# A two-block transformer step on one core: the operands of the 256-column products begin in the middle of a 64-byte line

## The chip, the cores and the metric

The kernel runs on one core of a Trainium2 chip. The core has TensorE (matrix products, PE in the profile, with the loads of the stationary operand listed apart as PEld), VectorE (DVE), ScalarE (ACT), GpSimd (POOL) and SyncE (SP, which here issues the loads). The metric is the device time of one execution in microseconds. The kernel before has a median of 2021.78 us in three runs (2020.27 to 2024.73).

## What is computed

Two transformer blocks on a sequence of 512 tokens with 1024 channels, all in fp32. Cut to the places that matter here:

```python
# block 1: three mixers behind one projection, then a gated FFN
proj = rmsnorm(x) @ w_in                        # pool input, q/k/v, cross q, three gates
merged = g0 * pool(...) + g1 * stick_breaking_attention(...) + g2 * cross_attention(...)
h = x + rmsnorm(merged @ w_out)
gu = rmsnorm(h) @ w_ffn_in                      # 1024 -> 2 x 2816
h = h + rmsnorm((silu(gu[:, :2816]) * gu[:, 2816:]) @ w_ffn_out)

# block 2, layer 0: gated recurrence (HGRN); layer 1: causal attention (MLA), 8 heads of 192
for layer in range(2):
    x = x + mixer[layer](rmsnorm(x))
    u = rmsnorm(x) @ w_up                       # 1024 -> 2 x 2816
    gate, up = split(conv3(u))                  # a causal convolution over 3 tokens
    x = x + (silu(gate) * up) @ w_down
```

So there are three FFNs. The causal attention adds a mask of 0 and -1e30 to its scores.

## The kernel before

**Products.** A product with fp32 precision is made of three float32r products on TensorE: each operand is split into a high part (a cast on ScalarE, line 63) and a low part (a subtraction on VectorE, line 66), and `mm3` (lines 114 to 116) multiplies high by high, high by low and low by high into the same PSUM bank. Each of them loads a stationary tile of 128 x 128 and streams 512 or 256 columns of a moving tile past it. Weights arrive as `raw` tiles (two buffers), and are split into tiles of the tag "w" (eight buffers): `whi` and `wlo` in `chunk`, `wu` in `seven`. Activations, transposed, are `XH` and `XL`, of 8 x 512 columns (`new_X`).

**Products over 256 columns.** The FFNs' up projections are done in part by a scheme that takes seven products of blocks where eight are usual (`seven`): sums of blocks of the weights (`u`, made on VectorE) meet sums of blocks of the activations. The sums of the activations are made once in `x_sums` and split into the tiles `xc` (eight buffers). One call of `seven` is 7 products of 4 x 3 TensorE products of 256 columns each; four of the seven take `xc` as moving operand, three take views of `XH` and `XL`. The first FFN does both halves (gate and up) by it, 20 calls; the other two do the gate by it, 10 calls each, and the up half by `projA`, over 512 columns, on the same `XH` and `XL`. The first pair of column blocks of each FFN runs in `projA_first`, in two halves of 256 columns, beside the normalisation that ends the mixer.

**Places in memory.** Pools lay tiles one behind the other in each of the 128 partitions. `fill` (line 81) takes some bytes at a pool's start, so that the tiles behind begin where they are meant to: 224, 320 and 224 bytes at the start of three pools (lines 364 to 366) and 480 in the pool of the causal attention (line 1245). With these, every operand of every TensorE product begins at a multiple of 64 bytes in its partition, the large ones at a multiple of 256.

**Masks.** The strict mask `negS` (for the stick-breaking attention of block 1) and the causal mask `negC` (for the attention of block 2) are both loaded at the start, cast, and kept to the end.

**Order.** The order on each engine follows the order in which the code issues, with a filler woven between the steps of a chain (`weave`); every engine works through its own row in order. Loads are issued by SyncE, each one waiting for its buffer to come free.

Of the kernel before, what the change touches and what calls it, by code (L numbers as in the profile page):

```python
# [10 lines left out]
F32 = mybir.dt.float32  # L11
F32R = mybir.dt.float32r
I32 = mybir.dt.int32
U8 = mybir.dt.uint8
AF = mybir.ActivationFunctionType
# [4 lines left out]
P = 128  # L20
D = 1024
S = 512
NT = S // P
KD = D // P
# [10 lines left out]
def kernel(ctx: ExitStack, tc: tile.TileContext, a: dict, out: bass.AP):  # L35
    nc = tc.nc
    uid = [0]

    def nm(s):
        uid[0] += 1  # L40
        return f"{s}_{uid[0]}"

    def pool(name, bufs=1, **kw):
        return tc.tile_pool(name=name, bufs=bufs, reuse_waits="tile", **kw)

    cp = ctx.enter_context(pool("cp"))
    wp = ctx.enter_context(pool("wp", bufs=2 * RING))
    gp = ctx.enter_context(pool("gp", bufs=2))
    sp = ctx.enter_context(pool("sp", bufs=6))
    sp_fill = ctx.enter_context(pool("sf"))  # L50
    yp = ctx.enter_context(pool("yp", bufs=6))
    ps = ctx.enter_context(pool("ps", space=PSUM))
# [5 lines left out]
    def row(s):  # L58

        return yp.tile([P, 512], F32, tag="y", name=nm(s))  # L60

    def act(out_, in_, func, **kw):
        return nc.scalar.activation(out=out_, in_=in_, func=func, **kw)  # L63

    def tt(out_, in0, in1, op):
        return nc.vector.tensor_tensor(out=out_, in0=in0, in1=in1, op=op)  # L66
# [10 lines left out]
    def load(dst, src):  # L77
        return nc.sync.dma_start(out=dst, in_=src)


    def fill(pool_, n):

        if n:
            nc.gpsimd.memset(pool_.tile([P, n // 4], F32, name=nm("fill")), 0.0)

    ident = cp.tile([P, P], F32, name="ident")
    mhalf = cp.tile([P, 8], F32, name="mhalf")
# [30 lines left out]
    def split(src, hi, lo):  # L118
        act(hi, src, AF.Copy)
        tt(lo, src, hi.bitcast(F32), ALU.subtract)  # L120
# [36 lines left out]
            if plain is not None:  # L157
                act(plain[:, hf * 4 : hf * 4 + 4, c0 : c0 + P], b.rearrange("p (k t) -> p k t", k=4), AF.Copy)

    def new_X(xp):  # L160
        return (
            xp.tile([P, KD, S], F32R, tag="XH", name=nm("XH")),
            xp.tile([P, KD, S], F32R, tag="XL", name=nm("XL")),
        )

    def open_pool(name, side="left"):
        g = tc.tile_pool(name=name, bufs=1, reuse_waits="tile", side=side)
        p_ = g.__enter__()
        return p_, lambda: g.__exit__(None, None, None)
# [3 lines left out]
    def run(g):  # L173
        for _ in g:
            pass
# [108 lines left out]
    def halves_of(T, j, l):  # L284
        return T.rearrange("p (c j) t -> p j c t", j=2)[:, j, :, l * 256 : (l + 1) * 256]

    def x_sums(X, plain, tmp, xp):

        B = {(j, l): halves_of(plain, j, l) for j in range(2) for l in range(2)}
        nT1, T3, nT2, T4 = (tmp[:, 2 * i : 2 * i + 2].rearrange("p k (u t) -> p (k u) t", u=2) for i in range(4))  # L290
        ops = {}

        def parts(key, src):
            t_ = [xp.tile([P, 4, 256], F32R, tag="xc", name=nm("xc"), bufs=8) for _ in range(2)]
            split(src, *t_)
            ops[key] = t_

        tt(nT1, B[0, 0], B[0, 1], ALU.subtract)
        parts("nT1", nT1)
        tt(T3, B[1, 1], B[0, 1], ALU.subtract)  # L300
        stt(nT2, T3, -1.0, B[0, 0], ALU.mult, ALU.subtract)
        parts("nT2", nT2)
        parts("T3", T3)
        stt(T4, nT2, -1.0, B[1, 0], ALU.mult, ALU.subtract)
        parts("T4", T4)
        for j, l in ((0, 0), (1, 0), (1, 1)):
            ops[j, l] = [halves_of(x_, j, l) for x_ in X]
        return ops

    def seven(w, col, ops, xp, dst, c21, done):  # L310

        A = []
        for i in range(2):
            raw = (wp, xp)[i].tile([P, KD, P], F32, tag="raw", name=nm("raw"), bufs=2)
            load(raw, w[:, col + i * P : col + (i + 1) * P].rearrange("(k p) n -> p k n", p=P))
            A.append([raw.rearrange("p (c j) n -> p j c n", j=2)[:, j] for j in range(2)])
        bY, bXZ = bank("Y"), bank("XZ")
        pY, pX, pZ = bY[:, :256], bXZ[:, :256], bXZ[:, 256:]  # L320
        lf, rt = slice(0, 256), slice(256, 512)

        def product(o, src, key, first):
            t_ = wp.tile([P, 2, 4, P], F32R, tag="w", name=nm("wu"))
            split(src, t_[:, 0], t_[:, 1])
            x_ = ops[key]
            for c in range(4):
                mm3(o, (t_[:, 0, c], t_[:, 1, c]), (x_[0][:, c], x_[1][:, c]), first and c == 0, c == 3, skip_group_check=True)

        def usum(a_, b_, o=None):  # L330
            if o is None:
                o = xp.tile([P, 4, P], F32, tag="u", name=nm("u"), bufs=2)
            tt(o, a_, b_, ALU.add)
            return o

        product(pY, A[0][0], (0, 0), True)
        act(dst[0][:, lf], pY, AF.Copy)
        yield 1
        u1 = usum(A[1][0], A[1][1])
        product(pX, u1, "nT1", True)  # L340
        u3 = usum(A[0][0], A[1][0], A[1][0])
        u2 = usum(u3, A[1][1])
        product(pY, u2, "nT2", False)
        act(dst[0][:, rt], pY, AF.Copy)
        product(pZ, A[0][1], (1, 0), False)
        tt(dst[0][:, lf], pZ, dst[0][:, lf], ALU.add)
        done(0, 0)
        product(pY, u3, "T3", False)
        act(dst[1][:, rt], pY, AF.Copy)
        stt(dst[1][:, rt], pX, -1.0, dst[1][:, rt], ALU.mult, ALU.subtract)  # L350
        done(1, 1)
        yield 1
        product(pY, A[1][1], "T4", False)
        c21(dst[1][:, lf], pY)
        product(pX, usum(u2, A[0][1], u2), (1, 1), False)
        tt(dst[0][:, rt], pX, dst[0][:, rt], ALU.add)
        done(0, 1)
# [3 lines left out]
    mem_in = a["mem"][0]  # L361
    w_in = a["w_in"][0]

    fill(cp, 224)
    fill(sp_fill, 320)
    fill(ctx.enter_context(tc.tile_pool(name="rf", bufs=1, reuse_waits="tile", side="right")), 224)
    RA, close_RA = open_pool("RA", "right")
    M, close_M = open_pool("mp")
    E1, close_E1 = open_pool("e1")
# [42 lines left out]

    negS_f = row("negS_f")[:, :P]
    load(negS_f, a["c_neg_strict"])
    negC_f = row("negC_f")[:, :P]
    load(negC_f, a["c_neg_causal"])
    identR = cp.tile([P, P], F32R, name="identR")
    act(identR, ident, AF.Copy)
    negS = cp.tile([P, P], F32R, name="negS")
    act(negS, negS_f, AF.Copy)  # L420
    negC = cp.tile([P, P], F32R, name="negC")
    act(negC, negC_f, AF.Copy)

    def copies(dst, n=S):
        def f(bs):
# [359 lines left out]
    H_, close_H = open_pool("hp")  # L785
    h = H_.tile([P, NT, D], F32, name="h")

    def out_proj(w, Y, nk, gpost, gnext, half0, nxt, plain=lambda: None, parts=None):

# [59 lines left out]
        if parts is None:  # L851
            g0 = projB(w, 0, Y, nk, d0)
            xpool = half0(g0)
            last = xpool is None
            Xn = None if last else new_X(xpool)
            run(g0)
            bs = [bank("B", f"c{t}") for t in range(NT)]
            for c in range(nch - RING):
                ch = getB(w, c, 512)
                for t in range(NT):  # L860
                    run(mmB(bs, t, c, ch, Y, nk))
            ends = [(bs, c, getB(w, c, 512), Y) for c in range(nch - RING, nch)]
        else:
            xpool = half0(None)
            last = xpool is None
            Xn = None if last else new_X(xpool)

            def pair_of(c):
                y_ = [parts.tile([P, 2, S], F32R, tag="xc", name=nm("yc"), bufs=8) for _ in range(2)]
                split(Y[:, 2 * c : 2 * c + 2], *y_)  # L870
                return y_

            b2 = [bank("B") for _ in range(NT)], [bank("B", f"c{t}") for t in range(NT)]
            bs = b2[1]
            for c in range(nch - 2):
                yc = pair_of(c)
                for hf in range(2):
                    ch = getB(w, c, hf * 512)
                    for t in range(NT):
                        run(mmB(b2[hf], t, c, ch, yc, nk, x0=2 * c))  # L880
            ycs = [pair_of(c) for c in (nch - 2, nch - 1)]
            ends = [(b2[hf], c, getB(w, c, hf * 512), ycs[c - nch + 2]) for hf in range(2) for c in (nch - 2, nch - 1)]
# [43 lines left out]
    def ffn_first(w):  # L926
        return lambda X_, pend: projA_first(
            w, (0, DFF), X_, (lambda b: sinks[0](b), lambda b: sinks[1](b)), pend, lambda: ff["mid"]()
        )


    w_fi = a["w_ffn_in"][0]
    for t in range(NT):
        load(h[:, t], x_in[t * P : (t + 1) * P])
    XA, close_XA = open_pool("xa")
    open_ff()
    X, steps = out_proj(
        a["w_out"][0], MG, KD, gain(a["norm_mix_post"][0]), gain(a["norm_ffn_pre"][0]),
        lambda g0: XA, ffn_first(w_fi), kept,
    )  # L940
    close_RA()

# [291 lines left out]
    )  # L1234


    L, close_L = open_pool("ml")
    g_c = gp.tile([P, 512], F32, tag="g", name=nm("g"))
    load(g_c[:, :256], a["mla_q_a_norm_2"][0].unsqueeze(0).to_broadcast([P, 256]))
# [2 lines left out]

    kr = L.tile([P, NT, 64], F32, name="kr")
    ssr = L.tile([P, NT], F32, name="ssr")
    fill(L, 480)
    cn = [None] * NT

    def c_norm(t, b, o):
# [249 lines left out]
```

## Time and profile before

| | kernel before |
|---|---|
| median of three runs | 2021.78 us (2020.27 to 2024.73) |
| the profiled execution | 2020.12 us |
| its span, first to last instruction | 2018.3 us |
| granted clock, mean | 0.997 of 2.4 GHz |
| TensorE busy | 1985.7 us, 98% of the span |
| VectorE busy | 1278.9 us, 63% |
| ScalarE busy | 960.2 us, 48% |

The span is cut into stages by what runs in them: the mixers of block 1 to 437 us, the first FFN's up projections to about 645, the recurrence from about 775 to 1095, the second FFN to about 1450, the attention to about 1656 and the third FFN to the end. "Busy" counts an instruction from its start to its end; the products on TensorE overlap each other, so their pace is read from the distance of their starts.

### The profile page before, as it was taken

What the parts mean: (1) busy time and instruction counts of PE and PEld (TensorE: products, weight loads), DVE (VectorE), ACT (ScalarE), POOL (GpSimd) and SP (SyncE); (2) the same over time, 40 slices, a digit from 0 to 9 for tenths busy, and PEclk for the clock granted to TensorE, in tenths of its full rate; (3) what the DMA queues carried; (4) which work ended last, traced back from release to release, by engine and by line L of the source; (5) the groups of instructions that cost most, each with busy time, mean ns of one, the idle gap of its engine ahead of it and who ended that gap; (6) DMA issues with size and microseconds to landing.
All of it is one profiled execution on the core that took longest, in us unless ns stands there. A gap on an engine that the chain in (4) does not pass through costs nothing.

```text
span 2018.3 us, 29724 instructions
## 1 busy us (share of the span) xinstructions
PE 1985.7 (98%) x11665; PEld 1717.8 (85%) x11665; DVE 1278.9 (63%) x2293; ACT 960.2 (48%) x1862; POOL 56.6 (3%) x88
## 2 busy tenths in 40 slices
PE   8999999999999999999999999999989999999999
PEld 6877788889999888888888999988877789999887
DVE  5664543489888326666556887853556459887632
ACT  5543452366555227333244555542367555555521
POOL 0000000000000000000010000000021000000000
PEclk9999999999999999999999999999999999999999
DMA  6232223324333322212212233233231123332322
GB/s 225 89 94 75 72 76 125 105 84 126 105 105 96 103 94 84 74 63 74 65 51 89 85 113 97 84 107 102 67 97 32 43 62 106 94 103 86 105 94 84
DMA packets 192482, 183.44 MB, mean 91 GB/s; under 512 B 6999, under 2 KB 159830, under 8 KB 192342
## 3 DMA queue, kind: packets, MB, share of 16 engines
q1 hardware_dynamic: 192342, 181.54, 29.0%
q8 instruction: 92, 1.51, 0.3%
q14 instruction: 48, 0.39, 0.1%
HBM read 179.42 MB, written 2.10 MB: 90 GB/s over the span
## 4 chain that ended last, share of the span: by engine, by line
PE 90%; DVE 4%; DMA 3%; ACT 2%; POOL 1%; issue 1%; SPq 0%; ACTq 0%; DVEq 0%; POOLq 0%
PE B L114 10%; PE B L116 10%; PE B L115 10%; PE A L114 9%; PE A L115 9%; PE A L116 9%; PE Y L114 4%; PE Y L116 4%; PE Y L115 4%; PE XZ L116 3%; PE XZ L114 3%; PE XZ L115 3%; PE hs L1108 2%; PE zt L92 1%; DVE wlo L66 1%; PE tr L92 1%
## 5 line engine op out<-in xcount | busy, mean ns | idle before, releaser
L66 DVE TENSOR_TENSOR wlo<-raw,whi 128x1024 fp32r<-128x1024 f32 (+2 forms) x217 | 257.3, 1188 | 335.7 <-ACT whi L63 335.1
L63 ACT ACTIVATE whi<-raw 128x1024 fp32r<-128x1024 f32 (+2 forms) x217 | 224.0, 1033 | 369.4 <-PE B L115 251.6
L114 PE MATMUL A<-XH,whi 128*128 128x512 f32 (+1 forms) x912 | 335.9, 369 | 0.0
L115 PE MATMUL A<-XL,whi 128*128 128x512 f32 (+1 forms) x912 | 330.4, 362 | 0.4 <-DVE XL L66 0.4
L116 PE MATMUL A<-XH,wlo 128*128 128x512 f32 (+1 forms) x912 | 329.3, 361 | 0.0
L114 PE MATMUL B<-whi,yc 128*128 128x512 f32 x528 | 205.8, 390 | 0.0
L115 PE MATMUL B<-wlo,yc 128*128 128x512 f32 x528 | 205.5, 389 | 0.0
L116 PE MATMUL B<-whi,yc 128*128 128x512 f32 x528 | 205.3, 389 | 0.0
L116 PEld LDWEIGHTS A<-XH,wlo 128*128 128x128 f32 x912 | 173.5, 190 | 26.4 <-issue 0.2
L114 PEld LDWEIGHTS A<-XH,whi 128*128 128x128 f32 x912 | 173.8, 191 | 23.8 <-ACT XH L63 0.2
L115 PEld LDWEIGHTS A<-XL,whi 128*128 128x128 f32 x912 | 173.9, 191 | 23.3 <-DVE XL L66 0.9
L114 PE MATMUL B<-whi,XH 128*128 128x512 f32 (+2 forms) x416 | 164.8, 397 | 0.9 <-ACT whi L63 0.9
L115 PE MATMUL B<-wlo,XH 128*128 128x512 f32 (+2 forms) x416 | 157.1, 378 | 1.1 <-DVE wlo L66 0.7
L116 PE MATMUL B<-whi,XL 128*128 128x512 f32 (+2 forms) x416 | 157.1, 379 | 0.0
L114 PE MATMUL Y<-xc,wu 128*128 128x256 f32 x480 | 136.0, 283 | 2.4 <-ACT g L63 2.1
L116 PE MATMUL Y<-xc,wu 128*128 128x256 f32 x480 | 135.8, 283 | 0.0
L115 PE MATMUL Y<-xc,wu 128*128 128x256 f32 x480 | 135.8, 283 | 0.0
L63 ACT ACTIVATE wu<-u 128x512 fp32r<-128x512 f32 x120 | 75.2, 628 | 98.5 <-PE A L115 61.9
L63 ACT ACTIVATE wu<-raw 128x512 fp32r<-128x512 f32 x160 | 98.8, 624 | 42.8 <-DMA raw<-in_ffn_w_up_dram 21.0
L114 PEld LDWEIGHTS B<-whi,yc 128*128 128x128 f32 x528 | 99.1, 188 | 20.8 <-issue 0.5
L116 PEld LDWEIGHTS B<-whi,yc 128*128 128x128 f32 x528 | 99.1, 188 | 20.6
L115 PEld LDWEIGHTS B<-wlo,yc 128*128 128x128 f32 x528 | 99.2, 188 | 20.2
(326 smaller groups left out, 4214.7 us busy)
## 6 DMA issues: line engine op xcount, KB each, us to landing
raw<-in_ffn_w_up_dram SPq DMA_DIRECT2D x88, 512.0 KB
raw<-in_w_ffn_in_dram SPq DMA_DIRECT2D x44, 512.0 KB
raw<-in_ffn_w_down_dram SPq DMA_DIRECT2D x44, 512.0 KB
raw<-in_w_in_dram SPq DMA_DIRECT2D x42, 512.0 KB
raw<-in_hgrn_w_in_dram SPq DMA_DIRECT2D x32, 512.0 KB
raw<-in_w_ffn_out_dram SPq DMA_DIRECT2D x22, 512.0 KB
raw<-in_w_out_dram SPq DMA_DIRECT2D x8, 512.0 KB
raw<-in_hgrn_w_out_dram SPq DMA_DIRECT2D x8, 512.0 KB
```

The source lines that it names most:

```text
L63: return nc.scalar.activation(out=out_, in_=in_, func=func, **kw)
L66: return nc.vector.tensor_tensor(out=out_, in0=in0, in1=in1, op=op)
L92: nc.tensor.transpose(dst_bank[:, k * P : (k + 1) * P], s_, ident)
L114: nc.tensor.matmul(out_, lhsT=sta[0], rhs=mov[0], start=first, stop=False, **kw)
L115: nc.tensor.matmul(out_, lhsT=sta[0], rhs=mov[1], start=False, stop=False, **kw)
L116: nc.tensor.matmul(out_, lhsT=sta[1], rhs=mov[0], start=False, stop=last, **kw)
L1108: nc.tensor.matmul(b[:, sl], lhsT=K[:, e, sl], rhs=Q[:, e, sl], start=True, stop=True)
```

## The change

The tiles `xc` and `wu` become views that begin 32 bytes into a tile that is 64 bytes longer (`wide`, with `HALF` = 8 elements of 4 bytes). The same is done to `XH` and `XL` where a call asks for it, which only the `out_proj` ahead of the first FFN does (`at=HALF`); there all products on them go over 256 columns. The `XH` and `XL` of the other FFNs, which products over 512 columns read too, stay where a tile begins. All tiles of the tag "w" share buffers, so `whi` and `wlo` lie in the longer ones too, at their start.

For the bytes that this takes, the pool `sp` of small tiles has five buffers instead of six, the two masks share a buffer (tag "neg"), so that the causal one is loaded and cast only at its mixer, and the fills shrink to 32 bytes each. The fill of 480 bytes in the attention's pool is dropped; some tiles behind it, operands of plain-fp32 products and of transposes, now begin at an odd multiple of 32 bytes. The operands of the products over 512 columns begin at multiples of 64 bytes, no longer all of 256.

```diff
-    sp = ctx.enter_context(pool("sp", bufs=6))
+    sp = ctx.enter_context(pool("sp", bufs=5))
...
-    def new_X(xp):
-        return (
-            xp.tile([P, KD, S], F32R, tag="XH", name=nm("XH")),
-            xp.tile([P, KD, S], F32R, tag="XL", name=nm("XL")),
-        )
+    HALF = 8
+
+    def wide(xp, tag, name, shape, at, **kw):
+        n = int(np.prod(shape))
+        t_ = xp.tile([P, n + 2 * HALF], F32R, tag=tag, name=name, **kw)[:, at : at + n]
+        ax = " ".join(f"a{i}" for i in range(len(shape)))
+        return t_.rearrange(f"p ({ax}) -> p {ax}", **{f"a{i}": v for i, v in enumerate(shape)})
+
+    def new_X(xp, at=0):
+        return tuple(wide(xp, t, nm(t), (KD, S), at) for t in ("XH", "XL"))
...
         def parts(key, src):
-            t_ = [xp.tile([P, 4, 256], F32R, tag="xc", name=nm("xc"), bufs=8) for _ in range(2)]
+            t_ = [wide(xp, "xc", nm("xc"), (4, 256), HALF, bufs=8) for _ in range(2)]
...
         def product(o, src, key, first):
-            t_ = wp.tile([P, 2, 4, P], F32R, tag="w", name=nm("wu"))
+            t_ = wide(wp, "w", nm("wu"), (2, 4, P), HALF)
...
-    fill(cp, 224)
-    fill(sp_fill, 320)
-    fill(ctx.enter_context(tc.tile_pool(name="rf", bufs=1, reuse_waits="tile", side="right")), 224)
+    fill(cp, 32)
+    fill(sp_fill, 32)
+    fill(ctx.enter_context(tc.tile_pool(name="rf", bufs=1, reuse_waits="tile", side="right")), 32)
...
-    negC_f = row("negC_f")[:, :P]
-    load(negC_f, a["c_neg_causal"])
...
-    negS = cp.tile([P, P], F32R, name="negS")
+    negS = cp.tile([P, P], F32R, tag="neg", name="negS")
...
-    negC = cp.tile([P, P], F32R, name="negC")
-    act(negC, negC_f, AF.Copy)
...
     X, steps = out_proj(
         a["w_out"][0], MG, KD, gain(a["norm_mix_post"][0]), gain(a["norm_ffn_pre"][0]),
-        lambda g0: XA, ffn_first(w_fi), kept,
+        lambda g0: XA, ffn_first(w_fi), kept, at=HALF,
     )
...
+    negC_f = row("negC_f")[:, :P]
+    load(negC_f, a["c_neg_causal"])
+    negC = cp.tile([P, P], F32R, tag="neg", name="negC")
+    act(negC, negC_f, AF.Copy)
     L, close_L = open_pool("ml")
...
-    fill(L, 480)
```

The products stand in the same order as before, but for a handful in the first 60 us. What moves is the causal mask. On ScalarE, at the hand-over from the second FFN to the attention, the casts of the last weights (`whi`), of the last two transposed blocks of `XH` and the first sums of squares (`cn`) stand in this order in the kernel before:

```order
L63 ACTIVATE XH_12553<-tr_13350 128x4x128
L63 ACTIVATE XH_12553<-tr_13357 128x4x128
L63 ACTIVATE junk_13377,ssa_13331<-h 128x512
L63 ACTIVATE whi_13465<-raw_13463 128x512
L63 ACTIVATE XH_12553<-tr_13431 128x4x128
L63 ACTIVATE XH_12553<-tr_13438 128x4x128
L63 ACTIVATE cn_13475,css_13476<-B_13399 128x256
```

And at the same place in the changed kernel:

```order
L63 ACTIVATE XH_12549<-tr_13346 128x4x128
L63 ACTIVATE XH_12549<-tr_13353 128x4x128
L63 ACTIVATE junk_13373,ssa_13327<-h 128x512
L63 ACTIVATE whi_13463<-raw_13461 128x512
L63 ACTIVATE negC<-negC_f_13383 128x128
L63 ACTIVATE XH_12549<-tr_13429 128x4x128
L63 ACTIVATE XH_12549<-tr_13436 128x4x128
L63 ACTIVATE cn_13473,css_13474<-B_13397 128x256
```

The mask's cast stands one place ahead of the casts of the last two blocks of `XH`. On SyncE's row of loads at the same hand-over (`raw` are weights of the attention's first projection, `gq` and `gk` small gains) the kernel before has

```order
L78 DMA raw_13463<-in_mla_w_in_dram 128x2x256
L78 DMA gq_13751<-in_mla_q_norm_dram 128x64
L78 DMA gk_13761<-in_mla_k_norm_dram 128x64
L78 DMA raw_13561<-in_mla_w_in_dram 128x2x320
L78 DMA raw_13567<-in_mla_w_in_dram 128x2x320
L78 DMA g_14048<-in_norm_ffn_dram 128x1024
```

and the changed kernel

```order
L78 DMA raw_13461<-in_mla_w_in_dram 128x2x256
L78 DMA gq_13749<-in_mla_q_norm_dram 128x64
L78 DMA gk_13759<-in_mla_k_norm_dram 128x64
L78 DMA raw_13559<-in_mla_w_in_dram 128x2x320
L78 DMA negC_f_13383<-in_c_neg_causal_dram 128x128
L78 DMA raw_13565<-in_mla_w_in_dram 128x2x320
L78 DMA g_14046<-in_norm_ffn_dram 128x1024
```

where the mask's load stands between two loads of weights.

## Rows read from the trace of the kernel before

**Rows 1.** The page's busy times by engine, and TensorE's granted clock in 40 slices.

```profile
PE 1985.7 (98%) x11665; PEld 1717.8 (85%) x11665; DVE 1278.9 (63%) x2293; ACT 960.2 (48%) x1862; POOL 56.6 (3%) x88
...
PEclk9999999999999999999999999999999999999999
```

**Rows 2.** The page's chain that ended last, by engine.

```profile
PE 90%; DVE 4%; DMA 3%; ACT 2%; POOL 1%; issue 1%; SPq 0%; ACTq 0%; DVEq 0%; POOLq 0%
```

**Rows 3.** TensorE's groups by form: count | busy us, mean ns of one | idle before.

```profile
L114 PE MATMUL Y<-xc,wu 128*128 128x256 f32 x480 | 136.0, 283 | 2.4 <-ACT g L63 2.1 <-ACT u L63 0.3
...
L114 PE MATMUL XZ<-XH,wu 128*128 128x256 f32 x320 | 90.6, 283 | 0.0
...
L114 PE MATMUL A<-XH,whi 128*128 128x256 f32 x256 | 74.3, 293 | 0.0
...
L1108 PE MATMUL hs<-Q,K 128*128 128x128 f32 x448 | 59.0, 274 | 0.0
...
L114 PE MATMUL XZ<-xc,wu 128*128 128x256 f32 x160 | 45.3, 283 | 0.0
```

**Rows 4.** Timeline of TensorE, first FFN: start us, length us, instruction; 168 steps.

```profile
579.79 0.28 PE L114 MATMUL Y<-xc,wu 128*128 128x256 f32 x1
579.91 0.28 PE L115 MATMUL Y<-xc,wu 128*128 128x256 f32 x1
...
599.95 0.28 PE L114 MATMUL Y<-xc,wu 128*128 128x256 f32 x1
```

**Rows 5.** Timeline of TensorE, last down projection, products over 512 columns; 67 steps.

```profile
1959.76 0.39 PE L115 MATMUL B<-wlo,yc 128*128 128x512 f32 x1
...
1974.95 0.39 PE L116 MATMUL B<-whi,yc 128*128 128x512 f32 x1
```

**Rows 6.** Timeline of TensorE, recurrence: plain-fp32 products over 128 columns, merged.

```profile
841.74 1.05 PE L1108 MATMUL hs<-Q,K 128*128 128x128 f32 x8
```

**Rows 7.** Timeline of TensorE, third FFN: from 512 columns to 256.

```profile
1696.55 0.39 PE L116 MATMUL A<-XH,wlo 128*128 128x512 f32 x1
1696.78 0.28 PE L114 MATMUL Y<-xc,wu 128*128 128x256 f32 x1
1696.89 0.28 PE L115 MATMUL Y<-xc,wu 128*128 128x256 f32 x1
1697.01 0.28 PE L116 MATMUL Y<-xc,wu 128*128 128x256 f32 x1
```

**Rows 8.** Timeline of all engines near 600 us: a weight load.

```profile
599.95 0.19 PEld L115 LDWEIGHTS Y<-xc,wu 128*128 128x128 f32 x1
```

**Rows 9.** Busy us by stretch: length, PE, PEld, DVE, ACT, POOL, clock, DMA.

```profile
437.00:500.00 63.00, 63.00 (x528) 63.00 (x527) 62.56 (x119) 40.19 (x76) 0.00 (x0) 1.00 0.34 102
500.00:645.00 145.00, 145.00 (x1211) 145.00 (x1210) 124.14 (x230) 85.24 (x168) 0.00 (x0) 1.00 0.33 99
1130.00:1310.00 180.00, 180.00 (x1123) 163.13 (x1122) 148.94 (x227) 100.60 (x166) 0.00 (x0) 1.00 0.34 104
```

**Rows 10.** Timeline of ScalarE: the mask's cast, and the hand-over to the attention.

```profile
22.54 0.31 ACT L63 ACTIVATE negC<-negC_f 128x128 fp32r<-128x128 f32 x1
...
1454.61 0.63 ACT L63 ACTIVATE whi<-raw 128x512 fp32r<-128x512 f32 x1
1458.66 1.33 ACT L63 ACTIVATE XH<-tr 128x512 fp32r<-128x512 f32 x2 [3.41 <-PE tr L92]
```

**Rows 11.** Timeline of SyncE's issues at the same hand-over.

```profile
1452.58 0.34 SPq L78 DMA_DIRECT2D gq<-in_mla_q_norm_dram  x1
1453.91 0.38 SPq L78 DMA_DIRECT2D raw<-in_mla_w_in_dram  x1
1456.74 0.38 SPq L78 DMA_DIRECT2D raw<-in_mla_w_in_dram  x1
```

**Rows 12.** Timeline of VectorE there: what waited for the small load.

```profile
1455.76 0.29 DVE L66 TENSOR_TENSOR tq<-cosT,gq 128x128 f32<-128x128 f32 x1 [0.62 <-DMA gq<-in_mla_q_norm_dram]
```

**Rows 13.** The strict mask's products: count, shortest/median/longest ns, first to last start us.

```profile
L521 PE MATMUL z<-negS,identR x32: 272/302/332, 53.3 to 232.7; 128*128 128x128 f32 x32
```

More of the change, by code (lines that the diff above doesn't have):

```diff
@@ L81, in fill @@
     def fill(pool_, n):
-        if n:
-            nc.gpsimd.memset(pool_.tile([P, n // 4], F32, name=nm("fill")), 0.0)
+        nc.gpsimd.memset(pool_.tile([P, n // 4], F32, name=nm("fill")), 0.0)
     ident = cp.tile([P, P], F32, name="ident")
@@ L786, with out_proj @@
     h = H_.tile([P, NT, D], F32, name="h")
-    def out_proj(w, Y, nk, gpost, gnext, half0, nxt, plain=lambda: None, parts=None):
+    def out_proj(w, Y, nk, gpost, gnext, half0, nxt, plain=lambda: None, parts=None, at=0):
         first = {}
@@ L854, in out_proj @@
             last = xpool is None
-            Xn = None if last else new_X(xpool)
+            Xn = None if last else new_X(xpool, at)
             run(g0)
@@ L865, in out_proj @@
             last = xpool is None
-            Xn = None if last else new_X(xpool)
+            Xn = None if last else new_X(xpool, at)
             def pair_of(c):
```

## The prediction

> **What bounds the kernel now.** I read the page's busy times and its chain first: TensorE is busy for 98% of the span [rows 1] and the chain that ended last runs through it for 90% [rows 2], at a granted clock of 1.00 in nearly every slice [rows 1]. So time comes or goes here almost only with the pace at which one product follows another. That pace is not in the groups of instructions: their 283 ns for a product over 256 columns is the length of one, and these overlap. The groups give the number and the kind [rows 3]. The pace is read from the starts in the timeline: in a stretch of products over 256 columns the starts at 579.79 and 599.95 us lie 168 steps apart, 120.0 ns each [rows 4]; over 512 columns those at 1959.76 and 1974.95 us lie 67 steps apart, 226.7 ns each [rows 5]. The difference, 106.7 ns for 256 columns, is one column per cycle of 2.4 GHz. What is left is the same in both, 120.0 - 106.7 = 13.3 ns per product, 32 such cycles. On this **excess** the prediction rests, since an operand's place in a line cannot change the columns.
>
> Two rows say what the excess is not. It is not the price of any change of the stationary tile: eight products of plain fp32 over 128 columns in 1.05 us, 274 ns long each [rows 3], follow each other at (1.05 - 0.27) / 7 = 111 ns [rows 6], and they too load 128 columns of 4-byte weights per product. So the load of a stationary tile allows 111 ns. Nor is it constant: the first product over 256 columns behind one over 512 starts at 1696.78 us, the next at 1696.89, and from there on the step is 0.12 again [rows 7]. With the same tiles at the same places a step of 0.11 us is possible when the work ahead was another. I read the excess as two readers of the same memory, the stream of moving columns and the load of the next stationary tile, which start at the same hundredth of a microsecond [rows 4, 8] and get in each other's way; the time at which each steps on to its next piece then matters, and so may the place where an operand begins.
>
> **The change, part by part.** In the kernel before every operand of every product begins at a multiple of 64 bytes (most at a multiple of 256). Afterwards the tiles xc and wu begin 32 bytes later, and XH and XL of the first FFN too. There are 3360 products of the seven-product scheme at 120 ns: 40 calls of `seven` times 84, which the groups add up to: three lines each of 480 and 320, six of 160, of which one each is shown [rows 3]. Of these 1680 are in the first FFN, with both operands shifted; in the two others 960 have both shifted (those on xc) and 720 only the stationary one (those on XH, XL). Of the 768 that TensorE runs on XH and XL with aligned weights (three lines of 256) [rows 3], the 192 of the first FFN's start have a shifted moving operand alone; the others keep their places.
>
> Both shifted, 2640 products. No row shows an operand off a multiple of 64, so the price is bounded from both sides. Below: 111 ns, the pace that the load of a stationary tile allows [rows 6], a gain of 9 ns each. Above: the excess is paid in pieces; if the 512 bytes of a stationary row are 8 lines of 64 bytes, a line costs 13.3 / 8 = 1.67 ns, a start in mid-line touches 9 lines instead of 8, and the moving row 17 instead of 16: 1.67 to 3.3 ns lost each. I take half of the excess back, 6.65 ns, since 106.7 + 6.65 = 113.3 ns is what the step of 0.11 us behind a product over 512 columns shows [rows 7], the nearest row there is. The reason is one of phase: the moving row is read at twice the rate of the stationary one, so with both begun in mid-line the first half line is used up after 8 cycles on the one side and 16 on the other, and the two no longer step on in the same cycle; begun at a line's start they do, every time.
>
> Not all of it reaches the end. From 437 to 500 us, where the first FFN's products run beside the angles of the rotary tables, VectorE is busy for 62.56 of 63.00 us [rows 9]: it cannot follow a faster TensorE there, and 63 / 0.120 = 525 products gain nothing. Behind that it is busy for 124.14 of 145.00 us and in the second FFN for 148.94 of 180.00 [rows 9], 86% and 83%: room for a TensorE that is 5.6% faster. So (2640 - 525) x 6.65 ns = **14.1 us less**.
>
> One shifted, 912 products: the phases differ by one half line in another way, and no row tells whether it helps. I take nothing; the ends are 9 ns gained and 1.67 ns lost, -8.2 to +1.5 us.
>
> Products over 512 columns keep places at a multiple of 64, though no longer of 256. In rows 5 the moving operand begins at a multiple of 512 bytes and the stationary one 256 further, and the products of rows 4, at other multiples of 256, have the same excess; odd multiples of 64 no row shows. I take nothing; a line's price each, 1.67 ns, would be 8.6 us on 5172 products. The plain-fp32 attention products of the second mixer, 144, and 144 transposes move to mid-line as well, because the fill of 480 bytes in their pool goes; the plain-fp32 pace of 111 ns [rows 6] is that of the loads, so I take nothing; at a full excess more for each they would cost 288 x 13.3 ns = 3.8 us.
>
> The causal mask. Its load, its row buffer and its cast leave the start (0.31 us of ScalarE at 22.54 us [rows 10]) and stand now in the hand-over to the second block's second mixer: on ScalarE ahead of the two casts of XH that TensorE waits for, on SyncE's load queue between two weight loads. In the trace those loads are issued at 1453.91 and 1456.74 us, each in 0.38 [rows 11]; the second waits for a buffer, so the mask's 64 KB would go out at about 1454.3. The small load issued at 1452.58 [rows 11] ended a wait of VectorE at 1455.76 [rows 12], 3.2 us later. The mask then lands at about 1457.5 and its cast ends at 1457.8. ScalarE is idle from 1455.2 until the casts at 1458.66, which wait for TensorE's transposes [rows 10]: the cast is hidden, with 0.8 us to spare. Without this cover it would cost what it is late, 0.3 us and more, with two casts of XH and the first sums of squares queued behind it. The buffer that the mask shares with the strict mask is last read at 232.7 us [rows 13], so nobody waits for it. Five instead of six small buffers in `sp`, and shorter fills: a small tile is written and read within a step or two of a loop, and I cost them at nothing. What comes late next in this hand-over is the load behind the cast, and it is not moved.
>
> The sum: 14.1 us less, all else nothing. The profiled execution took 2020.12 us around a span of 2018.3, so it would come to 2006.0; the median of the runs, 2021.78, lies 1.7 above it. From the median: 2021.8 - 14.1 = **2007.7 us**, said as 2008.
>
> A page would put the gain higher. The Trainium skill, "TensorE: Matmul & The Clock Gate", section Back-to-back issue gap, gives columns / 2.4 + 2.5 ns from product to product, 109.2 for 256; the trace has 120.0 instead, with loads between. If the shift brought that gap back, the sum would be 2115 x 10.8 ns = 22.8 us and the time 1999, an estimate by that page.
>
> **The rivals.**
> *Nothing changes.* The excess is a fixed price of handing the array from one 4-byte stream to the next, or the pieces read are 32 bytes or less. For it speaks that it is 13.3 ns at 256 and at 512 columns alike; against it, the step of 0.11 us [rows 7] and the 111 ns of rows 6. Time: 2022, within 2 us. The Trainium skill, "SBUF — State Buffer", section Specifications (TRN2), gives SBUF lines of 16 bytes; by that rule a row shifted by 32 bytes touches as many lines as before, and this rival holds. No row here shows a line's length.
> *A half line more is read.* The price of the upper bound above: 2640 x 3.3 + 912 x 1.67 ns = 10.2 us, at all 3552 products since TensorE is the bound there. Time 2032. It decides if the memory is read in lines of 64 bytes and each line costs its own collision, whatever the phase. For it speaks that 32 cycles divide evenly by 8 lines; if moving and stationary collide a second time per product, it would be as much again, 2042.
> *The whole gap closes* to 111 ns, for both kinds: (3552 - 525) x 9 ns = 27 us, 1995. Against it speaks VectorE, which at 86% would be near its limit.
> *The gain is bounded by VectorE* all through the first FFN: then only the 960 products of the other two gain, 6.4 us: 2015.
>
> **How the numbers follow.** Forecast (half the excess) 0.30, whole gap 0.10, VectorE as bound 0.10, nothing 0.22, a half line more 0.28. Faster by over 0.2% (about what a measurement of this kernel can tell from no change, 4 us): 0.50. Within: 0.22. Slower: 0.28. The range reaches from 1994 (whole gap) to 2036 (a half line more, and the mask or the small buffers some us late); of the slower case the part above it, with a second collision, is left out. If it is faster, 1994 to 2016.
>
> **What would show it.** In the profile after, the step between starts of products on xc and wu: 113 ns by the forecast, 120 by the first rival, 121.7 to 123.4 by the second, 111 by the third. The products on XH and wu of the second FFN tell the one-sided shift apart. The step of 512 columns must still be 226.7 ns, and VectorE's share from 500 us on must rise from 86 to some 90%. The mask's cast must stand before the casts of XH with idle time behind it. I am wrong if the step stays at 120.0 or grows, or if the step of 512 columns moves.

## The result and the profile after

The changed kernel is **slower by 0.68%**: 2035.7 us in the median (2034.74 to 2039.48) against 2022.67 us for the kernel before in the same comparison, a ratio of 1.0068 with a 95% interval of 1.0051 to 1.0086. The profiled execution took 2034.74 us around a span of 2032.8 us, 14.5 us more than the span before (2018.3).

Busy times, TensorE's clock and the chain, from the page of the changed kernel:

```profile
PE 2000.2 (98%) x11665; PEld 1713.2 (84%) x11665; DVE 1278.2 (63%) x2293; ACT 959.9 (47%) x1862; POOL 56.6 (3%) x87
...
PEclk9999999999999999999999999999999999999999
...
PE 88%; DVE 5%; ACT 2%; DMA 2%; issue 1%; POOL 1%; SPq 0%; POOLq 0%; ACTq 0%; DVEq 0%
```

Against [rows 1, 2] TensorE is busy for 14.5 us more, with the same 11665 products at the same clock; VectorE and ScalarE have not moved by 1 us. So the products follow each other more slowly. The same products as in [rows 4], 168 steps apart (start, length, instruction):

```profile
582.66 0.28 PE L113 MATMUL Y<-xc,wu 128*128 128x256 f32 x1
...
602.51 0.28 PE L113 MATMUL Y<-xc,wu 128*128 128x256 f32 x1
```

and as in [rows 5], 67 steps apart:

```profile
1973.35 0.40 PE L114 MATMUL B<-wlo,yc 128*128 128x512 f32 x1
...
1988.84 0.39 PE L115 MATMUL B<-whi,yc 128*128 128x512 f32 x1
```

Over 256 columns the step fell from 120.0 to 19.85 / 168 = **118.2 ns**. Over 512 columns, where no view was moved, it rose from 226.7 to 15.49 / 67 = **231.3 ns**. The steps also lost their evenness: before, nearly every product of 256 columns came 120 ns behind the last; afterwards nine in ten lie between 114 and 123 ns, in no fixed order. Counting the steps from start to start of all products by kind accounts for the whole difference:

| sum of the steps behind products | before | after | difference |
|---|---|---|---|
| on 512 columns (5171) | 1210.2 us | 1229.7 us | +19.5 |
| on 256 columns with `wu` (3360) | 405.7 | 401.0 | -4.7 |
| on 256 columns, others (1032) | 128.8 | 128.3 | -0.5 |
| the rest (plain fp32, transposes, waits between) | 261.7 | 262.0 | +0.3 |
| all | 2006.4 | 2021.0 | +14.6 |

The question is why products slow down whose views stayed at a tile's start.

### The profile page after: what moved, and what is told of

It reads as the page before. It is cut to its first block, busy times and chain, and to the rows that moved or that the text cites. A ratio compares the mean times of both kernels' runs of the same rounds, so it can differ in the third digit from the quotient of the medians.

```text
span 2032.8 us, 29733 instructions
## 1 busy us (share of the span) xinstructions
PE 2000.2 (98%) x11665; PEld 1713.2 (84%) x11665; DVE 1278.2 (63%) x2293; ACT 959.9 (47%) x1862; POOL 56.6 (3%) x87
## 4 chain that ended last, share of the span: by engine, by line
PE 88%; DVE 5%; ACT 2%; DMA 2%; issue 1%; POOL 1%; SPq 0%; POOLq 0%; ACTq 0%; DVEq 0%
PE B L113 10%; PE B L114 10%; PE B L115 10%; PE A L113 9%; PE A L114 9%; PE A L115 9%; PE Y L113 3%; PE Y L114 3%; PE Y L115 3%; PE XZ L114 3%; PE XZ L113 3%; PE XZ L115 3%; PE hs L1110 2%; PE zt L91 1%; PE tr L91 1%
## 5 line engine op out<-in xcount | busy, mean ns | idle before, releaser
L113 PE MATMUL B<-whi,yc 128*128 128x512 f32 x528 | 208.2, 394 | 0.0
L115 PE MATMUL B<-whi,yc 128*128 128x512 f32 x528 | 207.6, 394 | 0.0
```

Source lines behind the costliest of these rows:

```text
L113: nc.tensor.matmul(out_, lhsT=sta[0], rhs=mov[0], start=first, stop=False, **kw)
L115: nc.tensor.matmul(out_, lhsT=sta[1], rhs=mov[0], start=False, stop=last, **kw)
```

## The experiments

**The theories.** What did change for the 512-column products is where their tiles lie. The slots of the weight ring are 4160 bytes long instead of 4096, those of XH and XL 16448 instead of 16384, and the fills no longer round up to 256. Before, all of these operands stand at a multiple of 256; afterwards at 0, 64, 128 or 192 past one. *T1*: the pace hangs on how the places of the stationary and the moving operand stand to each other modulo 256; equal places give the even 226.7 and 120.0 ns, unequal ones more on 512 columns and less on 256. *T2*: the place inside a 64-byte line counts, the 32 bytes that the change is about. *T4*: the side edits (mask, sp, fills) cost the time. *T5*: not the places, but what ScalarE, VectorE or the transfers do beside them.

**The pace by itself (m1).** Streams of products and nothing else, all operands views of one long tile, `m` and `s` the bytes past a multiple of 256 of the moving and the stationary pair:

```python
for i in range(16):
    k = i % 8
    for u, v in ((0, 0), (0, 1), (1, 0)):                  # hi-hi, hi-lo, lo-hi
        nc.tensor.matmul(b[:, :n], lhsT=big[:, so[u] + k * 256 : so[u] + k * 256 + 128],
                         rhs=big[:, mo[v] + k * n : mo[v] + k * n + n], ...)
```

> This kernel leaves the two blocks out: it copies x to one long tile as fp32r and runs only streams of 48 products of 512 or of 256 columns in the pattern hi-hi, hi-lo, lo-hi, each with a weight load of 128x128, whose four operands lie at chosen numbers of bytes past a multiple of 256 within that tile; the four last streams of either width run beside copies on ScalarE and subtractions on VectorE. T1 (the pace hangs on how the addresses of the operands of one product, or of neighbouring products, stand to each other beyond 64 bytes): the streams with all operands at equal places show the 226.7 and 120.0 ns of before, those with 64, 128 or 192 bytes between operands show 230 to 233 ns and 114 to 118 ns. T2 (the place inside a 64-byte line counts): only streams whose operands lie at 32, 96, 160 or 224 differ from the others. T5 (the pace does not hang on the places of TensorE's own operands, but on what ScalarE, VectorE or the transfers do beside them): every stream without work beside it shows 226.7 and 120.0 ns, whatever the places.

The timeline of TensorE, merged; a stream's 48 steps end at the next stream's start. In the names, `wide` is 512 columns and `half` 256; M and S are followed by the places of the high and the low part, one letter for every 32 bytes: `a` is 0, `b` 32, `c` 64, `i` 256, `q` 512:

```profile
43.88 11.05 PE L56 MATMUL wideMaaSaax<-big 128*128 128x512 f32 x48
54.77 11.35 PE L56 MATMUL wideMaaSbbx<-big 128*128 128x512 f32 x48
65.96 11.36 PE L56 MATMUL wideMaaSccx<-big 128*128 128x512 f32 x48
77.16 11.40 PE L56 MATMUL wideMaaSddx<-big 128*128 128x512 f32 x48
...
132.95 11.04 PE L56 MATMUL wideMaaSiix<-big 128*128 128x512 f32 x48
143.83 11.04 PE L56 MATMUL wideMaaSqqx<-big 128*128 128x512 f32 x48
...
232.26 11.07 PE L56 MATMUL wideMbbSbbx<-big 128*128 128x512 f32 x48
243.16 11.25 PE L56 MATMUL wideMegSegx<-big 128*128 128x512 f32 x48
254.25 11.08 PE L56 MATMUL wideMaiSaix<-big 128*128 128x512 f32 x48
...
265.17 5.91 PE L56 MATMUL halfMaaSaax<-big 128*128 128x256 f32 x48
270.93 5.84 PE L56 MATMUL halfMaaSbbx<-big 128*128 128x256 f32 x48
276.60 5.82 PE L56 MATMUL halfMaaSccx<-big 128*128 128x256 f32 x48
282.26 5.79 PE L56 MATMUL halfMaaSddx<-big 128*128 128x256 f32 x48
...
389.90 11.36 PE L56 MATMUL wideBusyMaaSccx<-big 128*128 128x512 f32 x48
401.10 11.09 PE L56 MATMUL wideBusyMbbSbbx<-big 128*128 128x512 f32 x48
```

On 512 columns, equal places: 10.89 / 48 = 226.9 ns; the weights 32 bytes off 233.1, 64 bytes off 233.3; 256 bytes off 226.7 again. Both operands 32 bytes past a multiple of 256, and so equal: 227.1. On 256 columns: 120.0 at equal places, 118.1 at 32 bytes, 117.9 at 64. The other unequal pairs gave 229 to 234 ns on 512 columns and 117 to 120 on 256. So T1 has the directions; its sizes, 230 to 233 and 114 to 118 ns, were too narrow. T2 falls, since 64 acts as 32 does and a common 32 does nothing.

In the streams named `Busy` only VectorE was at work beside TensorE, not ScalarE as well. ScalarE's copies ran earlier, from 21 to 152 us, beside the first ten streams. Busy time of PE, PEld, DVE, ACT and POOL during `wideBusyMaaSccx`:

```profile
389.90:401.10 11.20, 11.20 (x49) 9.02 (x48) 10.89 (x10) 0.00 (x0) 0.00 (x0) 1.00 0.00 0
```

This stream, 64 bytes off, took 233.3 ns, as the one beside ScalarE did. T5 falls: `wideMegSegx`, with neither engine at work, took 11.09 / 48 = 231.0 ns, where T5 has 226.7.

**In the kernel (e1 to e3).** e1 is the changed kernel without the shift:

```diff
-        t_ = xp.tile([P, n + 2 * HALF], F32R, tag=tag, name=name, **kw)[:, at : at + n]
+        t_ = xp.tile([P, n + 2 * HALF], F32R, tag=tag, name=name, **kw)[:, 0:n]
```

> The changed kernel with every view moved back to the start of its tile: nothing lies at 32 bytes any more, but the tiles keep their 4160 and 16448 bytes, so that their places differ by multiples of 64 and not of 256. T1 (places that differ modulo 256 slow the products of 512 columns from 226.7 to about 231.5 ns and quicken those of 256 from 120.0 to about 118): as the changed kernel, 2031 to 2040 us, 512-column step 230 to 233 ns. T2 (the 32 bytes inside a line are what counts): back to before, 2019 to 2026 us, and the step on 256 columns back to 120.0 ns.

e3 is the kernel before with the side edits alone: `sp` with five buffers, the masks' move, and `fill(sp_fill, 352)`, which holds the places. The fill of 480 bytes in the attention's pool stays.

> The kernel before with only the side edits: causal mask loaded and cast where the changed kernel does it, in one shared buffer with the strict one, and five sp buffers; the fill behind sp is 352 bytes, so that all big tiles stay at a multiple of 256. T1 and T2: no difference, 2018 to 2026 us, steps 226.7 and 120.0 ns. T4: 2030 to 2040 us.

e2 is e3 with longer slots in the weight ring:

```diff
-            t_ = wp.tile([P, 2, 4, P], F32R, tag="w", name=nm("wu"))
+            t_ = wp.tile([P, 1024 + 16], F32R, tag="w", name=nm("wu"))[:, 0 : 1024].rearrange("p (h c n) -> p h c n", h=2, c=4)
```

> The kernel before with the causal mask loaded late and five sp buffers as in the changed one (to make room), and one thing more: the slots of the weight ring are 64 bytes longer (4160), so that its eight slots stand at 0, 64, 128 and 192 modulo 256 and every other tile of the big products stays at 0. No view is moved. T1: 512-column step 230 to 233 ns, so 5172 x 4 to 5 ns = 21 to 26 us more, 256-column step about 118 ns, so up to 9 us less; 2030 to 2042 us. T2: 2018 to 2026 us. T4 (the mask, the fills or the buffers cost the time): 2030 to 2040 us, but then e3 too.

| | median us | ratio to before, 95% interval | step on 256, on 512 columns (stretches of rows 4, rows 5) |
|---|---|---|---|
| changed kernel (before: 2022.7) | 2035.7 | 1.0068 (1.0051 to 1.0086) | 118.2, 231.3 ns |
| e1, shift undone, tiles long (before: 2024.1) | 2037.4 | 1.0065 (1.0048 to 1.0082) | 118.2, 231.3 |
| e2, weight ring's slots +64 bytes (2024.1) | 2030.1 | 1.0031 (1.0019 to 1.0044) | 116.5, 231.3 |
| e3, side edits alone (2024.1) | 2022.8 | 0.9998 (0.9987 to 1.0009) | 120.0, 226.7 |

Timeline of e1, the same products as above:

```profile
582.22 0.28 PE L113 MATMUL Y<-xc,wu 128*128 128x256 f32 x1
...
602.07 0.28 PE L113 MATMUL Y<-xc,wu 128*128 128x256 f32 x1
...
1976.34 0.40 PE L114 MATMUL B<-wlo,yc 128*128 128x512 f32 x1
...
1991.84 0.39 PE L115 MATMUL B<-whi,yc 128*128 128x512 f32 x1
```

The steps are those of the changed kernel, 19.85 and 15.50 us, though no view is shifted any more: the 32 bytes have no part in the result and T2 is out. With e3 T4 is out for the mask and the buffers; the fills that the change shrinks or drops act through the places that they set. In e2 one tag's slot length was changed and nothing else beyond e3:

```profile
580.50 0.28 PE L114 MATMUL Y<-xc,wu 128*128 128x256 f32 x1
...
600.08 0.28 PE L114 MATMUL Y<-xc,wu 128*128 128x256 f32 x1
...
1968.09 0.40 PE L115 MATMUL B<-wlo,yc 128*128 128x512 f32 x1
...
1983.59 0.39 PE L116 MATMUL B<-whi,yc 128*128 128x512 f32 x1
```

Against e3 its steps on 512 columns sum to 16.9 us more, those with `wu` to 8.8 less, the other 256-column ones to 2.7 less, the rest to 0.6 more: 6.0 us, the difference of the two spans (2027.2 and 2021.2). The loss on 512 columns is nearly all there; the gain on 256 is larger than in the changed kernel, since the streams' pace differs from place to place.

**What the displaced streams share, and what they don't (m2).** Finer offsets, narrower weights, other sets of places.

> Again no blocks, only streams of 48 products in the pattern hi-hi, hi-lo, lo-hi: places that differ by 4, 8, 16 and 48 bytes, weight loads of 96, 64 and 32 columns, hi and lo interleaved (the weights element by element, the moving operand in pieces of 16 or 32 elements), and more sets of four places, at 512 and 256 columns. T1: equal places 226.7 and 120.0 ns with 128 columns of weights; every stream with unequal places of 32 bytes or more off these two values, 512 columns above and 256 below. If the part above 213.3 and 106.7 ns (13.3 ns at equal places) is what the weight load takes from the moving operand, it shrinks with the columns of the weights: 10, 6.7 and 3.3 ns at 96, 64 and 32; if it is a cost of its own for each product, it stays at 13.3. Offsets of 4 to 16 bytes: open, 226.7 and 120.0 if the memory hands out whole pieces of 32 or 64 bytes.

Timeline; `aq` is 4 bytes, `aqq` 8; `One` loads 32 columns of weights:

```profile
42.61 11.05 PE L74 MATMUL wideMaaSaax<-big 128*128 128x512 f32 x48
53.50 11.32 PE L74 MATMUL wideMaaSaqaqx<-big 128*128 128x512 f32 x48
64.66 11.23 PE L74 MATMUL wideMaaSaqqaqqx<-big 128*128 128x512 f32 x48
...
221.00 11.28 PE L74 MATMUL wideOneMaaSaax<-big 128*32 128x512 f32 x48
232.12 11.28 PE L74 MATMUL wideOneMaaSccx<-big 128*32 128x512 f32 x48
243.24 5.91 PE L74 MATMUL halfMaaSaax<-big 128*128 128x256 f32 x48
```

Four bytes already break the even step: 11.16 / 48 = 232.5 ns on 512 columns. So a rule that rounds an operand's place down to 32 or 64 bytes is out; whether the memory is read in pieces at all, these streams do not tell. The other unequal sets gave 229 to 233 ns on 512 columns. On 256 most gave 116 to 119 ns, but five of them 119.7 to 120.7, where less than 120.0 was expected. With hi and lo interleaved in one tile 512 columns took up to 242.0 ns.

With 32 columns of weights the place no longer matters (231.7 ns at 0 and at 64 bytes); on 256 columns it doesn't with 64 columns of weights either (113.5 and 113.3 ns). Of the two prices expected for narrower weights, the one that shrinks with their columns fits 256 columns at first: the part above 106.7 ns is 9.4 ns with 96 columns of weights and 6.7 with 64, where 10 and 6.7 were expected. But it stays at 6.7 with 32, and on 512 columns the step at equal places rises from 226.7 to 230 and more. So neither price holds throughout. That fits a pace that hangs on how two streams fall into step better than a sum of collisions, but it is argued, not shown.

**Keeping the one and dropping the other (e4, e5, m3).** Slots of 4352 bytes keep every tile of the 512-column products at a multiple of 256, and `wu` alone moves inside its slot, by `AT` elements; four `sp` buffers and smaller fills make the room:

```diff
+            t_ = wp.tile([P, 1024 + 64], F32R, tag="w", name=nm("wu"))[:, AT : AT + 1024].rearrange("p (h c n) -> p h c n", h=2, c=4)
```

> wu32 keeps what the change wanted and drops what it cost: slots of the weight ring 256 bytes longer (4352), so that every tile of the 512-column products stays at a multiple of 256, and only the view wu, the weights of the products of the seven sums, 32 bytes into its slot. Four sp buffers and the side edits of e3 make the room. Beside it goes e5_wu64 with the same edit at 64 bytes, a whole line. T1: 512-column step 226.7 ns as before; the 3360 products with wu at 118.4 ns (the stream with the weights 32 bytes off showed that) in place of 120.0, 5 us less: 2014 to 2020 us. T2 in its first form (a shift of one operand halves the gap or does nothing): 2008 or 2022 us.

> As e4_wu32, with wu 64 bytes into its slot: it keeps its place in the 64-byte line, and only its place modulo 256 differs from the moving operand's. T1: 512-column step 226.7 ns, products with wu at about 117.8 ns, 3360 x 2.2 = 7 us less, of which some hides in stretches that VectorE bounds: 2013 to 2019 us. T2 (place inside the line): no difference from before, 2019 to 2026 us.

> No blocks again: streams of 60 products of 256 columns with the very addresses of the seven sums (weights wu of 2 x 4 x 128 in slots of 4352 bytes, moving operand the two tiles xc, or the halves of XH and XL), the weights at 0, 4, 8, ... 252 bytes past a multiple of 256. T1: 120.0 ns at 0 alone, 115 to 119 ns at nearly all others, 4 and 8 bytes among them; a few may be near 120 by chance. T2: 120.0 ns at 64, 128 and 192 too, and a lower value only off a line's edge, with a period of 64 bytes.

Beside 2021.8 us for the kernel before, e4 (32 bytes) took 2018.1 us, ratio 0.9984 (0.9975 to 0.9993). e5 (64 bytes) 2015.7 us, ratio 0.9966 (0.9955 to 0.9978). The step on 512 columns is 226.7 ns in both, that in the stretch of [rows 4] 118.3 and 117.8. A shift by 64 bytes does what one by 32 does, slightly better. No run has the longer slots with `AT` = 0; what the slots and the four buffers do by themselves is read from the products that aren't on `wu`, whose steps sum to 1.9 us more in e4 than before, and to 3.3 us more in e3, without the longer slots. In m3, streams with the addresses of the seven sums, the number in the name is the offset in bytes, one letter for each digit (`aaa` 0, `aae` 4, `aii` 88); `sum` has `xc` as the moving operand, `xt` XH and XL:

```profile
34.88 7.36 PE L48 MATMUL sumAtaaax<-big 128*128 128x256 f32 x60
42.08 7.26 PE L48 MATMUL sumAtaaex<-big 128*128 128x256 f32 x60
...
190.43 6.98 PE L48 MATMUL sumAtaiix<-big 128*128 128x256 f32 x60
197.25 7.26 PE L48 MATMUL sumAtajcx<-big 128*128 128x256 f32 x60
...
453.18 6.99 PE L48 MATMUL xtAtaiix<-big 128*128 128x256 f32 x60
460.01 7.21 PE L48 MATMUL xtAtajgx<-big 128*128 128x256 f32 x60
```

120.0 ns at 0, and at 88 bytes 6.82 / 60 = 113.7 ns and 6.83 / 60 = 113.8 for the two kinds (113.3 once settled). Most offsets gave 116.5 to 119.5 ns; T1's "120.0 at 0 alone" was too strong, since about a quarter of the offsets came out at 119.8 to 121.7 as well, most of them as a mean of uneven steps. Each offset ran once for each kind, so the best is the best seen.

**The best offset, and the 512 columns (e6, m4).**

> As e4 and e5, with wu 88 bytes into its slot, the offset at which the streams with both moving operands of the seven sums ran at 113.3 ns, steadily (113 and 114 ns alternating). T1: 512-column step 226.7 ns, the 3360 products with wu near 113.3 in place of 120.0 ns where PE runs undisturbed: 6.7 ns x (3360 - 525 that VectorE bounds) = 19 us, less if every pause throws the pair of streams out of step: 2002 to 2012 us. T2: 24 bytes into a line after a whole line, so as 24 bytes; no number of its own, but it has no reason for it to beat 32 and 64.

> No blocks: the products with the addresses of the two projections, all tiles of the weight ring shifted together by 0, 4, ... 252 bytes against the tiles of X. First 64 streams with the weights as the stationary operand (512 columns), then 64 with the weights as the moving one, then 32 with 256 columns. T1: 226.7 ns at 0; 228 to 236 ns at nearly all other offsets; for 256 columns 120.0 ns at 0 and 113 to 120 elsewhere. Open: whether some offset gives the 512 columns a steady step under 226.7, 220.0 if half of the 13.3 ns goes as it does for 256 columns at 88 bytes; if there is one for both projections, the whole ring may be shifted by it.

e6, `AT` = 22: **2008.1 us**, beside 2023.0 for the kernel before, ratio 0.9926 (0.9912 to 0.9940), faster than both kernels. Timeline in its third FFN, 55 steps on `wu`, and the stretch of [rows 5]:

```profile
1847.24 0.28 PE L115 MATMUL Y<-XL,wu 128*128 128x256 f32 x1
...
1853.47 0.28 PE L116 MATMUL Y<-xc,wu 128*128 128x256 f32 x1
...
1953.47 0.39 PE L115 MATMUL B<-wlo,yc 128*128 128x512 f32 x1
...
1968.66 0.39 PE L116 MATMUL B<-whi,yc 128*128 128x512 f32 x1
```

6.23 / 55 = 113.3 ns, and 15.19 / 67 = 226.7 ns. In the second and third FFN 81 and 87% of the steps on `wu` are 113 or 114 ns, in the first only 34%; in the stretch of [rows 4] they are 116.7 ns, evenly. One offset can have several steady paces. e5, with 64 bytes, shows it within its first FFN:

```profile
479.07 0.28 PE L114 MATMUL Y<-xc,wu 128*128 128x256 f32 x1
...
504.46 0.28 PE L116 MATMUL XZ<-XH,wu 128*128 128x256 f32 x1
...
529.40 0.28 PE L116 MATMUL XZ<-XH,wu 128*128 128x256 f32 x1
...
644.94 0.28 PE L116 MATMUL Y<-xc,wu 128*128 128x256 f32 x1
```

The first two lines lie 224 steps apart, 113.3 ns each; the last two 981 steps, 117.8 ns each. The kind of product and the places modulo 256 are the same, and there are short pauses of TensorE between the two stretches. So unequal places alone do not fix the pace. What picks one of its values behind a pause is open.

In e6 the steps on `wu` sum to 9.7 us less than before, all others to 3.2 us more (e3: 3.3 us more). The medians differ by 14.9: the profiled execution, at 2013.82 us, was the slowest of the five, while that of the kernel before, at 2020.12, was as fast as the fastest of its runs.

m4 shifts the whole weight ring against X. As stationary operand on 512 columns the weights settled at 226.7 ns at 0 and at six other offsets (120, 132, 144, 156, 228, 252 bytes), elsewhere they ran at 228 to 237; as moving operand they settled at 226.7 at 0 alone and took up to 240. No offset was under 226.7, so none of these beats the places of before:

```profile
756.00 11.06 PE L45 MATMUL movAtaaatx<-big 128*128 128x512 f32 x48
766.90 11.56 PE L45 MATMUL movAtaaetx<-big 128*128 128x512 f32 x48
778.30 11.37 PE L45 MATMUL movAtaaitx<-big 128*128 128x512 f32 x48
```

(227.1 ns at 0, 237.5 at 4 bytes.)

## Why the prediction was wrong

**The bound was right.** The time followed the pace of TensorE's products alone, and the prediction's way to read it, from start to start, is what showed the change.

**The step that failed is the one on the products over 512 columns.** It saw that they "keep places at a multiple of 64 though no longer of 256", said that no row shows odd multiples of 64, and took nothing, with 8.6 us as an end. Measured: +19.5 us, 3.8 ns on each of 5171 products; m1 shows the place as the cause and e2 the slot length in the kernel. The error was to ask about each operand's place in a line. All rows of before showed one state, equal places modulo 256, and that the same excess stood at 256 and 512 columns was a property of this state. An end taken from it could not bound another.

**The gain on 256 columns was real, but small and for another reason.** Forecast: 6.65 ns on 2640 products, for both operands in mid-line. Measured: 1.8 ns in the stretch of [rows 4], 4.7 us over all 3360, shifted on one side or both, and the same step of 118.2 ns with the shift undone (e1). The prediction's argument from phase had both operands begun in mid-line fall out of step; m1 shows that a common 32 bytes changes nothing, and that they must lie differently to each other. The one-sided 912, taken as nothing, gained nearly as much: those of the second and third FFN 1.3 ns each. The forecast's 113.3 ns, read off the step of 0.11 us in [rows 7], does exist, at 64 and at 88 bytes and for part of the products, not at 32.

**VectorE's limit was not there.** The prediction let 525 products from 437 to 500 us gain nothing, because VectorE was busy for 62.56 of 63.00 us there [rows 9]. The stretch of the same 528 products, in the changed kernel and in e6 (its length, then the busy time of PE, PEld, DVE, ACT and POOL):

```profile
441.70:504.20 62.50, 62.35 (x528) 62.15 (x527) 61.83 (x116) 40.05 (x76) 0.00 (x0) 1.00 0.36 102
437.70:499.30 61.60, 61.31 (x528) 61.11 (x527) 61.20 (x114) 39.41 (x75) 0.00 (x0) 1.00 0.34 101
```

They took 62.5 and 61.6 us in place of 63.0, and their steps on `wu` are 118.2 and 115.3 ns without the pauses, as short as behind them. A VectorE at 99% did not hold these back. The term, 525 x 6.65 ns = 3.5 us, decided nothing. Behind it VectorE's share rose from 86 to 87%, not to 90, since the gain was small.

**The mask and the small edits: right.** The mask's cast on ScalarE stands where it was expected and is covered, with 0.44 us of idle time behind it:

```profile
1468.44 0.31 ACT L63 ACTIVATE negC<-negC_f 128x128 fp32r<-128x128 f32 x1 [2.35 <-DMA negC_f<-in_c_neg_causal_dram]
1469.19 1.33 ACT L63 ACTIVATE XH<-tr 128x512 fp32r<-128x512 f32 x2 [0.44 <-PE tr L91]
```

e3 puts the mask's move and the five buffers together at 0.9998. The plain-fp32 products, which the dropped fill moved, show no loss (the rest of the steps, theirs among them: +0.3 us).

**The rivals.** "A half line more is read" (2032) came near the time, and by the wrong mechanism: it had the steps on `xc` and `wu` grow to 121.7 to 123.4 ns, and they fell. "Nothing changes" has the 32 bytes right and misses the tiles' length. The range, to 2036, just holds the time, through that rival and not through its own reason. The text's own test decided: it named a step of 512 columns that moves as what would make it wrong.

**The two pages.** The Trainium skill, "SBUF — State Buffer", section Specifications (TRN2), gives lines of 16 bytes; no run here shows a line of any length, and m2's streams change their pace at 4 bytes. The Trainium skill, "TensorE: Matmul & The Clock Gate", section Back-to-back issue gap, would give an estimate of 109.2 ns for 256 columns by its formula for an isolated product; no stream here came below 113.3.

**What stays open** is the mechanism: which reads of the two operands meet, and why the relation repeats after 256 bytes. The pair that the prediction named, the row that streams and the load of the next stationary tile, cannot be all of it: in m1's `wideMegSegx` every load begins at the same place modulo 256 as the row that streams beside it, and the step is 231.0 ns. The narrow weights of m2 fit neither of the two prices throughout. A stream without a weight load between its products was not tried.

## What to carry to other kernels

Where TensorE sets the time, the slot length of a pool is part of the kernel: lengthening a tag by a few bytes moves every tile that shares it or lies behind it, and here (e2) it cost 17 us on products whose code did not change, 6 us with what the shorter ones gained. For these products, with 4-byte operands and a weight load each, keep the operands of long streams equal modulo 256, and try short streams at unequal places by measuring, since the best offset seen (88 bytes here) follows from no rule found. When every row of a trace shows one and the same state, it bounds nothing outside of that state: say so, and widen the range by what the whole group of instructions could pay.

## What was not expected of the hardware

- The pace of these products depends on how their operands' places differ modulo 256, down to 4 bytes: on 512 columns 226.7 ns at equal places, 228 to 240 at nearly all others.
- The same displacement works in opposite directions: on 256 columns the 120.0 ns at equal places are slower than most offsets (the slowest gave 121.7), and 113.3 is the best seen.
- Unequal places do not fix the pace alone: with the same 64 bytes e5 held 113.3 ns over 224 products and 117.8 over 981, in one FFN.
- Fewer columns of weights do not make a long stream faster: 231.7 ns with 32 columns of weights on 512, against 226.9 with 128 at equal places.
